# A state space layer turns its scan's inputs and outputs from SBUF to SBUF, without DRAM between

## The chip, the core and the metric

The kernel runs on one core of a Trainium2 chip. The metric is the device time of one execution in microseconds (us); a time without a unit below is in us. The core's engines are TensorE (PE, matrix products), VectorE (DVE), ScalarE (ACT), GpSimd (POOL) and SyncE (SP, which here only issues DMA transfers). Each engine works through its own instructions in order, and an instruction waits on semaphores for what it needs. A DMA is issued by an instruction on SP, ACT or POOL and is then carried out by the core's 16 DMA engines. SBUF is the memory on the core with 128 partitions, PSUM the one that PE writes to, and DRAM lies outside.

## The reference, cut to what matters

The program is a stack of layers on 512 tokens of 1024 channels in float32: a mixer of pooling and a gated delta rule, a feed-forward block, an attention layer with selected blocks, and last a state space layer with 64 groups of 16 channels and 64 complex states each. The change is in the last one:

```python
def _s5_mixer(h, w_in, log_dt, ..., d_skip, w_glu, w_out):
    u, z = jnp.split(h @ w_in, 2, axis=-1)
    u = u.astype(f32).reshape(bsz, seq, G, C)
    ...
    bu = B u                  # per group: 16 channels to 64 complex states
    x[t] = a * x[t-1] + bu[t] # the scan over the 512 tokens
    y = Re(C x) + d_skip * u
    y = jax.nn.gelu(y.reshape(bsz, seq, SSM_WIDTH))
    ga, gb = jnp.split(y @ w_glu, 2, axis=-1)
    y = ga * jax.nn.sigmoid(gb)
    y = y * jax.nn.silu(z)
    return y @ w_out
```

(The two lines on bu and x stand for several of the reference's.) The result is added to h, and a last norm follows.

## The kernel before

**Products and jobs.** All dense products go through one stream of passes (`Kit.steps`). A job is one column block of a weight matrix, 1024 by 128. It is fetched by one DMA of 512 KB (`raw`, L99, on SP's queue), split into a high and a low part (`hi` on ACT, L105, `lo` on DVE, L106), and then multiplied with the 8 tiles of the input in 24 matmuls of 128x512 (L132: per tile hi by hi, hi by lo, lo by hi). At the start of a job the one after the next is fetched, and the next one is split. What was handed to `K.after` is issued there too. In the layer the jobs are `wu` 0 to 7 (the inputs u), `wz` 0 to 7 (the gates z, whose result goes to `sz`), then 16 `wglu` and 8 `wout`. The layer begins with 70 of these matmuls (`LEAD` 36 + 34) beside the norm of the layer's input; once its factor `rstd` is there, PE goes on.

**The scan's blocks.** A block b of the eight is 128 channels, that is, one `wu` job. For each block:

- u = product times rstd (DVE L1851, `u`, 128 channels by 512 tokens). It is written to a DRAM tile `D1` (L214, issued through `K.after`), and read back in another shape by `chunks` (L1846): `Uc` has a partition for each of 8 pieces of 16 rows, and 512 values in it.
- `state(b)`: 32 short matmuls `pw` on Uc (PE L1777), and a chain on DVE (L1783 to L1796: two products m1 and m2, a sum, two scan instructions `Z`, two products m3 and m4, and a difference that gives `Xs`).
- `toeplitz(b)`: the tile `T` of the block, in 8 DMAs of 64 KB from a prepared DRAM tile `DK` (L1761), even ones on SP, odd ones on ACT.
- `output(b)`: 16 matmuls of Uc with T (PE L1810), 32 of Xs with a prepared tile `made` (PE L1817), into the bank `py`; ACT copies it to `yt` (L1819). `made` is loaded by POOL three blocks ahead.
- `finish(b)`: four transposes of yt (PE L1827), a copy `yc` (ACT L1829), and a write of yc to a DRAM tile `D2` (ACT L1830).
- `back(b)`: D2 is read into a tile `sq` of 128 by 512 (SP L1964); `outputs(b)`: GELU and a split into `yh` and `yl` (L1969), the inputs of the `wglu` products.

**What sets the order.** SP and PE run in the order in which the code is written (`MANUAL`); on DVE, ACT and POOL the scheduler of the compiler orders the instructions before the program is built. Between the steps of a block the code runs passes of the products: 384 matmuls for `wu` and `wz`, of which 70 are the lead, `SPARE` = 46 follow, `TAIL` = 24 stand behind the last block, and the rest is spread evenly over the 31 gaps between the steps. The code of block b does, in this order: chunks(b+2), state(b+1), toeplitz(b+1), a gap, the T part of output(b), a gap, its Xs part, a gap, finish(b), a gap, then back(b-1) and outputs(b-2). Ahead of block 0 stand chunks(0), chunks(1), toeplitz(0) and state(0). Buffers: three `u`, three `Uc`, two `T`, two `Xs`, three PSUM banks for products.

**Semaphores of the DMAs.** The DMAs of SP and ACT share eight semaphores in turn, so that an issue on either queue also waits until the one eight before it, over both queues together, has landed.

## Time and profile before

| | us |
|---|---|
| median of 3 runs (lowest to highest) | 1347.67 (1347.02 to 1347.9) |
| the profiled execution | 1349.54 |
| its span in the trace | 1347.4 |
| the layer's stretch in it, from the first products after the norm to the end | 1073 to 1347 |
| the eight blocks of the scan in it | 1086 to 1189 |
| first `wglu` product | 1196.5 |

The profile is a record of one execution: when each instruction began, how long it took, what the engine waited for ahead of it, and when each DMA landed. A row of a timeline has the start, the duration in us, the engine, the line, the operation, what it writes and reads, the shape and the count of instructions run together; in square brackets stands the idle time ahead of it and what ended it. The duration of a matmul is longer than the distance to the next one, since they overlap. Line numbers are those of the kernel before; in the kernel after, the same lines of the layer stand a few lower.

### The profile page before, as it was taken

To read this page: it belongs to the slowest core of one execution; us is meant where nothing else is said; L and a number is where in the kernel's file an instruction comes from. 1 tells how busy PE (TensorE), PEld (TensorE's weight loads), DVE (VectorE), ACT (ScalarE), POOL (GpSimd) and SP (SyncE) were. 2 spreads that over 40 slices of the span, in tenths; PEclk is the share of its full clock that TensorE was granted. 3 is DMA by queue.
4 is the path that set the end of the run, shared out by engine and by line. 5 is a ranking of instruction groups with operands and counts; after the bars stand their busy time and mean duration, and the time that the engine had idled before them with its cause. 6 is when DMAs were issued, how large, how long until landed. Compare 5 with 4: busy or idle time off the path is not lost.

```text
span 1347.4 us, 22525 instructions
## 1 busy us (share of the span) xinstructions
PE 1289.7 (96%) x8360; PEld 1041.2 (77%) x8360; DVE 934.4 (69%) x2163; ACT 548.1 (41%) x1167; POOL 414.5 (31%) x456
## 2 busy tenths in 40 slices
PE   8899989999998999999999999999999999899997
PEld 5677766887886888888888777887877777678896
DVE  8867785558978768768775667777876665624365
ACT  5233222334322333333434546655765322333364
POOL 5723442130015566654220003443553100003200
PEclk9899999999998999999999999999999999999998
DMA  5111101143332344444445754312005379733331
GB/s 192 42 54 33 33 32 44 48 128 98 95 141 79 127 158 144 143 144 166 141 135 157 203 163 126 95 48 79 17 18 191 104 217 282 200 100 98 94 110 63
DMA packets 81197, 152.94 MB, mean 114 GB/s; under 512 B 23840, under 2 KB 46000, under 8 KB 79936
## 3 DMA queue, kind: packets, MB, share of 16 engines
q1 hardware_dynamic: 71408, 130.46, 31.0%
q0 software_dynamic: 2688, 15.75, 3.5%
q10 hardware_dynamic: 6992, 5.30, 1.5%
q8 instruction: 66, 1.08, 0.3%
q14 instruction: 43, 0.35, 0.1%
HBM read 119.60 MB, written 21.40 MB: 105 GB/s over the span
## 4 chain that ended last, share of the span: by engine, by line
PE 75%; DVE 13%; issue 3%; DMA 3%; ACT 3%; POOL 2%; SPq 0%; DVEq 0%; ACTq 0%; POOLq 0%
PE ps L132 53%; PE ps L1886 3%; DVE lo L106 3%; PE pa L1206 3%; PE acc L1303 2%; PE pt L1264 2%; PE pv L1087 2%; DMA T<-DK 1%; DVE xlbuf L237 1%; ACT P L1215 1%; PE pb L578 1%; PE hid L1119 1%; DMA sq<-D 1%; PE py L1817 1%; PE pu L587 1%
## 5 line engine op out<-in xcount | busy, mean ns | idle before, releaser
L105 ACT CAST hi<-raw 128x512 fp32r<-128x512 f32 x357 | 203.1, 613 | 351.2 <-PE ps L132 238.1
L106 DVE TENSOR_TENSOR lo<-raw,hi 128x512 fp32r<-128x512 f32 x357 | 274.9, 795 | 80.6 <-ACT hi L105 80.3
L132 PE MATMUL ps<-xlbuf,hi 128*128 128x512 f32 x736 | 302.9, 412 | 4.4 <-DVE xlbuf L237 4.3
L132 PE MATMUL ps<-xhbuf,hi 128*128 128x512 f32 x736 | 301.9, 410 | 3.7 <-ACT hi L105 2.7
L132 PE MATMUL ps<-xhbuf,lo 128*128 128x512 f32 x736 | 299.1, 406 | 4.3 <-DVE lo L106 4.3
L132 PEld LDWEIGHTS ps<-xhbuf,hi 128*128 128x128 f32 x736 | 140.4, 191 | 38.5 <-issue 5.1
L132 PEld LDWEIGHTS ps<-xhbuf,lo 128*128 128x128 f32 x736 | 140.9, 191 | 35.4 <-DVE lo L106 6.7
L132 PEld LDWEIGHTS ps<-xlbuf,hi 128*128 128x128 f32 x736 | 140.2, 190 | 35.5 <-DVE xlbuf L237 7.2
L1220 POOL TENSOR_TENSOR P<-P,sm 128x128 f32<-128x128 f32 (+3 forms) x128 | 96.3, 773 | 189.3 <-DVE sm L1218 138.2
L132 PE MATMUL ps<-hh,hi 128*128 128x512 f32 x256 | 100.5, 393 | 0.0
L132 PE MATMUL ps<-hh,lo 128*128 128x512 f32 x256 | 99.7, 390 | 0.0
L132 PE MATMUL ps<-hl,hi 128*128 128x512 f32 x256 | 99.7, 389 | 0.0
L1215 ACT ACTIVATE P<-P,nm 128x128 f32<-128x128 f32 (+3 forms) x128 | 71.8, 563 | 57.7 <-DVE nm L1214 50.5
L1214 DVE CUSTOM_DVE_ANT_0 P<-pa,nc 128x128 f32<-128x128 f32 (+3 forms) x128 | 60.2, 484 | 9.9 <-PE pa L1206 7.5
L1644 POOL TENSOR_TENSOR F<-keep 128x512 f32<-128x512 f32 x32 | 42.0, 1334 | 80.7 <-PE pt L1672 50.4
L1644 POOL TENSOR_TENSOR V<-keep 128x576 f32<-128x576 f32 x32 | 45.3, 1436 | 35.9 <-DMA DM<-V 35.4
L132 PEld LDWEIGHTS ps<-hh,hi 128*128 128x128 f32 x256 | 48.1, 188 | 10.6 <-issue 0.8
L132 PEld LDWEIGHTS ps<-hh,lo 128*128 128x128 f32 x256 | 48.1, 188 | 10.0
L132 PEld LDWEIGHTS ps<-hl,hi 128*128 128x128 f32 x256 | 48.1, 188 | 9.7
L132 PE MATMUL ps<-yh,hi 128*128 128x512 f32 x128 | 50.6, 396 | 0.9 <-ACT hi L105 0.9
L132 PE MATMUL ps<-yh,lo 128*128 128x512 f32 x128 | 50.7, 396 | 0.0
L1264 PE MATMUL pt<-ident,P 128*128 128x128 f32 x320 | 47.1, 274 | 3.8 <-POOL P L1220 1.7
(557 smaller groups left out, 2546.8 us busy)
## 6 DMA issues: line engine op xcount, KB each, us to landing
raw<-in_wup_dram SPq DMA_DIRECT2D x32, 512.0 KB, 3.6
raw<-in_wdown_dram SPq DMA_DIRECT2D x32, 512.0 KB, 3.6
made<-DM POOLq DMA_DIRECT2D x8, 1472.0 KB, 8.1
raw<-in_win_dram SPq DMA_DIRECT2D x19, 512.0 KB, 3.5
raw<-in_s_wglu_dram SPq DMA_DIRECT2D x16, 512.0 KB, 3.5
DM<-V SPq DMA_DIRECT2D x8, 576.0 KB, 3.0
DM<-Wt SPq DMA_DIRECT2D x8, 512.0 KB, 2.9
raw<-in_n_kv_dram SPq DMA_DIRECT2D x8, 512.0 KB, 4.0
```

Source lines behind the costliest of these rows:

```text
L105: self.nc.scalar.copy(hi[:, s], raw[:, s])
L106: self.nc.vector.tensor_tensor(lo[:, s], raw[:, s], hi[:, s].bitcast(F32), ALU.subtract)
L132: mm(ps, w[:, s], xs[k][x], start=k == 0 and n == 0, stop=k == kt - 1 and n == 2)
L1087: mm(R["v"][i], x[k][:, i * 128:i * 128 + 128], w[:, s], start=k == 0 and n == 0, stop=k == 7 and n == 2)
L1206: mm(pa[g2][:, 0:lead + nk], QS[gp][:, g2, i, r, :], keys[b][:, gp * 2 + g2, key0:AT[b] + nk], start=n == 0, stop=n == 1)
L1214: v.tensor_tensor_reduce(P[g2][:, 0:nk], pa[g2][:, lead:lead + nk], pos[:, 512 - nk:512], -slope, 3e38, ALU.add, ALU.min, nm[:, g2:g2 + 1])
L1215: act.activation(P[g2][:, 0:nk], P[g2][:, 0:nk], AF.Exp, scale=-1.0, bias=nm[:, g2:g2 + 1], accum_out=sm[:, g2:g2 + 1])
L1220: p.tensor_tensor(P[g2][:, 0:nk], P[g2][:, 0:nk], sm[:, g2:g2 + 1].to_broadcast([128, nk]), ALU.mult)
L1264: nc.tensor.transpose(pt[:, s], P[g2][:, s], ident)
L1303: mm(o[halves[g2], q * 128:q * 128 + 128], Vt[:, j, c:c + 64], T[g2][:, s], start=fresh and (q, j) == (0, 0), stop=(b, q, j) == (1, 3, i), ...
L1644: eng.tensor_tensor(o[:, x:x + 4], self.S[f][:, js, b * 8 + x:b * 8 + x + 4].rearrange("p j x -> p x j")[:, :, :, None].to_broadcast([128, ...
L1886: nc.tensor.matmul(banks[m][:, 0:256], w[:, s], os[k][x][:, a * 256:a * 256 + 256], start=k == 0 and n == 0, stop=k == 7 and n == 2)
```

## The change

The DRAM tiles D1 and D2 and `chunks` go. When u of a block is there, eight DMAs on SP (through `K.after`) carry it from SBUF to SBUF: piece j takes 64 columns of all 128 partitions (32 KB) and puts them into 16 partitions of Uc. The way back is alike: `back(b)` carries yc to `sq` in eight DMAs of 32 KB on SP, from 16 partitions each; ACT no longer issues a write. `back(b)` now stands directly behind the steps of block b, and outputs(b-1) ahead of it. There are five Uc and two u instead of three each; m3 and m4 use the buffers of m1 and m2. From `wu` 4 on, the jobs of `wu` and `wz` alternate. SPARE is 36, and 8 passes (`APART`) stand between state(0) and the steps of block 0.

```diff
--- before.py
+++ after.py
@@ -1373,7 +1373,7 @@
 FIRST, EACH = 490, 60
 NORM, BACK = 20, 170
 LEAD = 36, 34
-SPARE = 46
+SPARE, APART = 36, 8
 TAIL = 24
 TWO_PI = 2.0 * math.pi
 MAGIC = 1.5 * 2.0 ** 23
@@ -1729,11 +1729,8 @@
         def pool(name, bufs, **kw):
             return stack.enter_context(tc.tile_pool(name=name, bufs=bufs, reuse_waits="tile", **kw))
 
-        self.sd = pool("sd", 1, space=bass.MemoryType.DRAM)
         self.sp = sp = pool("sp", 1)
         self.sps = pool("sps", 2, space=PSUM)
-        self.D1 = [self.sd.tile([128, 512], F32, name=f"D1{b}") for b in range(8)]
-        self.D2 = [self.sd.tile([128, 512], F32, name=f"D2{b}") for b in range(8)]
         self.sw = pool("sw", 2)
         self.rho = sp.tile([128, 64], F32, name="rho")
         nc.gpsimd.dma_start(self.rho, self.P.rho)
@@ -1788,8 +1785,8 @@
         for x in range(2):
             v.tensor_tensor_scan(Z[:, x], df, m1[:, x], 0.0, ALU.mult, ALU.add)
         X = self.Xs[b % 2]
-        m3 = sw.tile([128, 2, 256], F32, name="m3", bufs=1)
-        m4 = sw.tile([128, 2, 256], F32, name="m4", bufs=1)
+        m3 = sw.tile([128, 2, 256], F32, tag="m1", name="m3", bufs=1)
+        m4 = sw.tile([128, 2, 256], F32, tag="m2", name="m4", bufs=1)
         v.tensor_tensor(m3, Z, Cb, ALU.mult)
         v.tensor_tensor(m4, Z[:, ::-1], Sf, ALU.mult)
         m3v, m4v = (t.rearrange("p x (g n) -> p (x g) n", g=4) for t in (m3, m4))
@@ -1825,9 +1822,8 @@
         for g in range(4):
             gs = slice(g * 128, g * 128 + 128)
             nc.tensor.transpose(py[:, 1, gs], self.yt[:, gs], self.K.ident)
-        yc = sw.tile([128, 2, 4, 64], F32, name="yc", bufs=1)
-        nc.scalar.copy(yc, py[:, 1].rearrange("p (g h n) -> p h g n", g=4, h=2))
-        nc.scalar.dma_start(self.D2[b], yc.rearrange("p h g n -> p (h g n)"))
+        self.yc = sw.tile([128, 2, 4, 64], F32, name="yc", bufs=1)
+        nc.scalar.copy(self.yc, py[:, 1].rearrange("p (g h n) -> p h g n", g=4, h=2))
         yield
 
     def run(self, wcol, stack, first, last):
@@ -1841,15 +1837,14 @@
         yh, yl = (szp.tile([128, 8, 512], F32R, name=n) for n in ("yh", "yl"))
         R, held, ys, os, ga, silu, kept_w, banks, sums, got = {}, [], [], [], {}, {}, {}, {}, {}, {}
 
-        def chunks(b):
-            self.Uc[b] = self.sw.tile([128, 8, 64], F32, name="Uc", bufs=3)
-            nc.sync.dma_start(self.Uc[b].rearrange("p g n -> p (g n)"), self.D1[b])
-
         def inputs(b):
             def done(ps):
-                u = self.sw.tile([128, 512], F32, name="u", bufs=3)
+                u = self.sw.tile([128, 512], F32, name="u", bufs=2)
                 nc.vector.tensor_tensor(u, ps, R["rstd"], ALU.mult)
-                K.after(nc.sync.dma_start, self.D1[b].rearrange("(j c) (g n) -> (c g) j n", j=8, n=64), u.rearrange("p (j n) -> p j n", j=8))
+
+                self.Uc[b] = self.sw.tile([128, 8, 64], F32, name="Uc", bufs=5)
+                for j in range(8):
+                    K.after(nc.sync.dma_start, self.Uc[b][j * 16:j * 16 + 16].rearrange("p g n -> p (g n)"), u[:, j * 64:j * 64 + 64])
             return K.xs, K.hold(R, held, done)
 
         def gates(m):
@@ -1961,7 +1956,9 @@
         def back(b):
 
             y = got[b] = K.work.tile([128, 512], F32, tag="sq", name="sq")
-            nc.sync.dma_start(y.rearrange("p (j n) -> p j n", j=8), self.D2[b].rearrange("(j c) (g n) -> (c g) j n", j=8, n=64))
+            yc = self.yc.rearrange("p h g n -> p (h g n)")
+            for j in range(8):
+                nc.sync.dma_start(y[:, j * 64:j * 64 + 64], yc[j * 16:j * 16 + 16, :])
 
         def outputs(b):
 
@@ -1977,7 +1974,9 @@
                 first[b].products = [inputs(b)]
             else:
                 K.queue(W["wu"][b], [inputs(b)])
-        for m in range(8):
+            if b > 3:
+                K.queue(W["wz"][b - 4], [gates(b - 4)])
+        for m in range(4, 8):
             K.queue(W["wz"][m], [gates(m)])
         for m in range(8):
             K.queue(W["wglu"][m], [glu(m, 0)], lambda: len(ys) == 8, cut=(2, 7) if m == 0 else None)
@@ -1987,8 +1986,6 @@
         K.queue(None, [out(m, 1) for m in range(8)])
 
         def side(b):
-            if b + 2 < 8:
-                chunks(b + 2)
             if b + 1 < 8:
                 self.state(b + 1)
                 self.toeplitz(b + 1)
@@ -2003,24 +2000,20 @@
             K.lead(K.norm_steps(wcol, R, permute=True), R, held, *LEAD)
             K.norm_bank = None
             K.run(SPARE)
-            chunks(0)
-            chunks(1)
             self.toeplitz(0)
             self.state(0)
+            K.run(APART)
             steps = 8 * 4 - 1
-            left = 384 - sum(LEAD) - SPARE - TAIL
+            left = 384 - sum(LEAD) - SPARE - APART - TAIL
             for b in range(8):
                 for _ in side(b):
                     n = left // steps
                     left, steps = left - n, steps - 1
                     K.run(n)
                 if b > 0:
-                    back(b - 1)
-                if b > 1:
-                    outputs(b - 2)
-            back(7)
+                    outputs(b - 1)
+                back(b)
             K.run(TAIL)
-            outputs(6)
             outputs(7)
             self.inner.close()
             with tc.tile_pool(name="so", bufs=2, reuse_waits="tile") as so, \
```

**SP, from the end of the lead to the T tile of the second block.** Numbers behind names count tiles, and a count at the end of a row is of equal instructions in a row; DK0 belongs to block 0. Before:

```order
L214 DMA D10_10823<-u_11025 128x8x64
L214 DMA D11_10824<-u_11027 128x8x64
L214 DMA D12_10825<-u_11031 128x8x64
L99 DMA raw_11077<-in_s_wu_dram 128x1024
L214 DMA D13_10826<-u_11069 128x8x64
L1846 DMA Uc_11101<-D10_10823 128x512
L1846 DMA Uc_11103<-D11_10824 128x512
L1761 DMA T_11105<-DK0_2988 16x8x128 x4
L1846 DMA Uc_11145<-D12_10825 128x512
L1761 DMA T_11178<-DK1_2989 16x8x128 x4
```

And after:

```order
L214 DMA Uc_11009<-u_11007 16x8x64 x8
L214 DMA Uc_11012<-u_11010 16x8x64 x8
L214 DMA Uc_11017<-u_11015 16x8x64 x8
L99 DMA raw_11084<-in_s_wu_dram 128x1024
L214 DMA Uc_11077<-u_11075 16x8x64 x8
L1758 DMA T_11105<-DK0_2988 16x8x128 x4
L1758 DMA T_11184<-DK1_2989 16x8x128 x4
L99 DMA raw_11208<-in_s_wz_dram 128x1024
L214 DMA Uc_11201<-u_11199 16x8x64 x8
```

Before, one write of u of block 3 and two reads stand ahead of the four T transfers of block 0 (T_11105). After, the eight pieces of Uc of each of blocks 0 to 3 do, those of block 3 (from u_11075) right ahead of T_11105.

**DVE, from the splits beside the lead's end to the end of the first chain.** In the first rows `lo` belongs to weight jobs; ps_11044 (before) and ps_11050 (after) are the product of the fourth `wu` job. Before:

```order
L1851 TENSOR_TENSOR u_11031<-ps_10996,rstd_11023 128x512
L106 TENSOR_TENSOR lo_11034<-raw_10994,hi_11033 128x512 x2
L1851 TENSOR_TENSOR u_11069<-ps_11044,rstd_11023 128x512
L106 TENSOR_TENSOR lo_11072<-raw_11039,hi_11071 128x512 x2
L1783 TENSOR_TENSOR m1_11132<-pw_11115,made_10854 128x512
L1784 TENSOR_TENSOR m2_11133<-pw_11115,made_10854 128x512
L1785 TENSOR_TENSOR m1_11132<-m1_11132,m2_11133 128x512
L1789 SCALAR_TENSOR_TENSOR Z_11137<-dec0_10844,m1_11132 128x256 x2
L1793 TENSOR_TENSOR m3_11140<-Z_11137,made_10854 128x512
L1794 TENSOR_TENSOR m4_11141<-Z_11137,made_10854 128x512
L1783 TENSOR_TENSOR m1_11165<-pw_11148,made_10856 128x512
L1796 TENSOR_TENSOR Xs0_10847<-m3_11140,m4_11141 128x8x63
```

And after:

```order
L106 TENSOR_TENSOR lo_11019<-raw_10976,hi_11018 128x512 x2
L106 TENSOR_TENSOR lo_11079<-raw_11024,hi_11078 128x512 x2
L1843 TENSOR_TENSOR u_11015<-ps_10978,rstd_11005 128x512
L1780 TENSOR_TENSOR m1_11132<-pw_11115,made_10836 128x512
L1781 TENSOR_TENSOR m2_11133<-pw_11115,made_10836 128x512
L1782 TENSOR_TENSOR m1_11132<-m1_11132,m2_11133 128x512
L1786 SCALAR_TENSOR_TENSOR Z_11137<-dec0_10826,m1_11132 128x256 x2
L1790 TENSOR_TENSOR m3_11140<-Z_11137,made_10836 128x512
L1791 TENSOR_TENSOR m4_11141<-Z_11137,made_10836 128x512
L1793 TENSOR_TENSOR Xs0_10829<-m3_11140,m4_11141 128x8x63
L1843 TENSOR_TENSOR u_11075<-ps_11050,rstd_11005 128x512
```

Before, u of block 3 (u_11069) stands ahead of the chain of block 0 (m1_11132 to Xs0). After, it (u_11075) stands behind that chain, and u of block 2 (u_11015) behind two more splits.

**SP, at the end of the scan.** Before:

```order
L99 DMA raw_11973<-in_s_wz_dram 128x1024
L1964 DMA sq_12026<-D25_10836 128x8x64
L99 DMA raw_12046<-in_s_wglu_dram 128x1024
L1964 DMA sq_12099<-D26_10837 128x8x64
L1964 DMA sq_12104<-D27_10838 128x8x64
L99 DMA raw_12112<-in_s_wglu_dram 128x1024
```

And after:

```order
L99 DMA raw_12044<-in_s_wz_dram 128x1024
L1961 DMA sq_12099<-yc_12085 128x1x64 x8
L99 DMA raw_12123<-in_s_wglu_dram 128x1024
L1961 DMA sq_12178<-yc_12164 128x1x64 x8
L99 DMA raw_12193<-in_s_wglu_dram 128x1024
```

The second `wglu` fetch (raw_12112 before, raw_12193 after) stands behind the read of block 7 from D2 before, behind eight pieces from yc of block 7 after; between the last transposes and the first wglu pass PE has 32 passes in both.

**PE.** From the end of the lead, 44 passes stand ahead of pw of block 0 before, none between it and pw of block 1, and 7 ahead of the T part of output(0). After, the counts are 34, 8 and 7.

## Rows read from the trace of the kernel before

**Rows 1.** The page: the chain of work that ended last, shares by engine.
```profile
PE 75%; DVE 13%; issue 3%; DMA 3%; ACT 3%; POOL 2%; SPq 0%; DVEq 0%; ACTq 0%; POOLq 0%
```

**Rows 2.** Windows: stretch, its length, busy of PE, PEld, DVE, ACT, POOL; PEclk, DMA share, GB/s.
```profile
1100.00:1150.00 50.00, 47.85 (x457) 37.47 (x455) 31.58 (x50) 15.00 (x27) 2.12 (x4) 1.00 0.93 275
1200.00:1250.00 50.00, 50.00 (x216) 40.13 (x215) 18.09 (x26) 18.49 (x32) 11.88 (x9) 1.00 0.30 95
```

**Rows 3.** Waits of PE, 1084 to 1200: who waited for whom, us, times, longest.
```profile
PE py L1827 <- ACT yt L1819: 4.6, 2, 3.4
PE pw L1777 <- DVE m L1784: 1.4, 1, 1.4
PE py L1810 <- DMA T<-DK: 1.0, 1, 1.0
PE ps L132 <- ACT hi L105: 0.9, 1, 0.9
PE pw L1777 <- DMA Uc<-D: 0.8, 1, 0.8
```

**Rows 4.** Line 1761: issue time ns min/median/max, a waiter, and issue to landing.
```profile
L1761 SPq DMA_DIRECT2D T<-DK x32: 555/600/1928, 1083.1 to 1170.2; - x32
...
  ACT yt L1819: 7.2, 1
...
DMA to landing us min/median/max: 2.5/4.7/11.1
```

**Rows 5.** Timeline of PE from the restart behind the norm.
```profile
1073.09 0.73 PE L132 MATMUL ps<-xhbuf,hi 128*128 128x512 f32 x1 [0.94 <-DVE u L1851]
...
1076.61 0.39 PE L132 MATMUL ps<-xhbuf,lo 128*128 128x512 f32 x1
1076.84 0.40 PE L132 MATMUL ps<-xhbuf,hi 128*128 128x512 f32 x1
...
1085.72 1.15 PE L1777 MATMUL pw<-Uc,made 128*64 128x64 f32 x32 [0.75 <-DMA Uc<-D]
...
1091.19 1.09 PE L1810 MATMUL py<-T,Uc 128*64 128x128 f32 x16
...
1128.79 1.09 PE L1810 MATMUL py<-T,Uc 128*64 128x128 f32 x16 [0.95 <-DMA T<-DK]
...
1165.49 1.11 PE L1827 MATMUL py<-ident,yt 128*128 128x128 f32 x4 [3.37 <-ACT yt L1819]
```

**Rows 6.** Windows, columns as in rows 2: behind the restart and behind the longest wait.
```profile
1073.00:1076.50 3.50, 3.41 (x8) 2.74 (x9) 2.43 (x5) 0.34 (x1) 0.00 (x0) 0.53 0.64 157
1165.40:1168.00 2.60, 2.51 (x8) 2.22 (x9) 0.70 (x2) 0.63 (x2) 0.00 (x0) 0.50 1.19 287
```

**Rows 7.** Timeline of DVE: u of block 3, then the chain's first and last instruction.
```profile
1080.48 0.69 DVE L1851 TENSOR_TENSOR u<-ps,rstd 128x512 f32<-128x512 f32 x1 [5.05 <-PE ps L132]
...
1086.91 0.69 DVE L1783 TENSOR_TENSOR m<-pw,made 128x512 f32<-128x512 f32 x1 [4.54 <-PE pw L1777]
...
1092.08 0.67 DVE L1796 TENSOR_TENSOR Xs<-m,m 128x504 f32<-128x504 f32 x1
```

**Rows 8.** Issue time on SP by line, ns min/median/max; the attention layer's K, then D1.
```profile
L981 SPq DMA_DIRECT2D K<-hi x16: 461/594/672, 761.6 to 827.5; - x16
L214 SPq DMA_DIRECT2D D<-u x8: 360/392/1061, 1073.1 to 1122.4; - x8
```

**Rows 9.** Tile K, 760 to 830: issue to landing of transfers of 128 KB.
```profile
DMA to landing us min/median/max: 2.2/2.3/4.3
```

**Rows 10.** The chain of waits ahead of the `wglu` products: start, us, step.
```profile
1189.41 0.60 ACT yc L1829
1190.03 2.02 DMA D<-yc
...
1192.58 4.88 DMA raw<-in_s_wglu_dram
```

**Rows 11.** The page's DMA issues: count, KB each, median us to landing.
```profile
raw<-in_s_wglu_dram SPq DMA_DIRECT2D x16, 512.0 KB, 3.5
```

## The prediction

> **What bounds the kernel now.** I read the shares of the chain of waits first: PE carries 75% of it [rows 1], so a us counts where PE loses it. The layer's stretches come next: in the first 50 us behind the scan PE is busy all the time, inside the scan for 47.85 of 50, with the DMA engines at 0.93 [rows 2]. Behind the scan nothing is idle to take up a delay: what PE loses ahead of the first `wglu` product shows at the end in full. The waits of PE in the scan are few: 4.6 on the copy yt (two times, 3.4 the longest), 1.4 on DVE's m, 1.0 on T, 0.8 on Uc, and 0.9 on a weight split at the start of the `wglu` jobs [rows 3]. The clock adds to that: the granted clock is 0.50 (the 1.2 GHz level) in the 2.6 us behind the longest wait, and 0.53 behind the restart that follows the norm [rows 6]. All this is some 10 us, and so the most that the change can take away in this layer.
>
> **What is taken away.** D2's write leaves ACT, D1's reads and writes leave SP. The long yt waits come from ACT, which stood in an issue of T ahead of the copy (7.2 us put down to it [rows 4]); an issue also waits for the DMA eight before it, and D1 and D2 put large transfers among those. With pieces of 32 KB in their place, and block b's pieces ahead of T(b+2), I take these waits as gone, and also those for Uc, m and T, since pw and the T part now come at other times: 4.6 + 1.4 + 1.0 + 0.8 = 7.8 [rows 3], and half of the 2.6 us at half clock [rows 6], 1.3. **Gain 9.1**, and hardly more, as only the restart's slow start and the 0.9 are left. If the yt waits stay, 4.6 + 1.3 of it are not had (a rival, below). The products are as many as before in another order, and the gates need nothing that is late; five Uc and the shared m buffers cost nothing, as the chain writes m3 behind the sum that reads m1 and m2. Two u instead of three make u(2) wait for all pieces of Uc(0): it matters for state(2) alone, a block later, which covers it. ACT's half of T(0) has no new wait ahead of it.
>
> **What is added: a wait at the start of the scan.** This term decides. By the order of DVE, u(3) now stands behind the whole chain of state(0). By the order of SP, the eight pieces of Uc(3) stand ahead of SP's four transfers of T(0). An issue that waits holds all that is behind it, so T(0) waits for state(0), and the T part of output(0), early on PE, waits for T(0). In times of the trace of before, where the restart is at 1073.09:
>
> 1. Eight passes behind the restart take 1076.61 - 1073.09 = 3.52, the next ones 0.23 each [rows 5]. pw(0) stands behind 34: 1073.09 + 3.52 + 26 x 0.23 = 1082.6. Uc(0) is there by then: eight issues of 0.59 (below) from 1073.1 end at 1077.8, and a landing of up to 4.7 ends at 1082.5.
> 2. The chain begins 1.19 behind the start of pw (1085.72, 1086.91) and took 1092.08 + 0.67 - 1086.91 = 5.84 with an instruction of the next chain in it of 0.69 [rows 5, 7]: 5.15 without. 1082.6 + 1.2 + 5.15 = 1088.95.
> 3. u(3) takes 0.69 [rows 7]: 1089.6.
> 4. Eight issues of its pieces. No row shows such a piece. The nearest by form is a transfer on SP over all partitions in a long row of issues, K at 0.59 in the middle and 0.67 at most; the lowest is the write of u to D1 at 0.39 [rows 8]. I take 0.59, nearest in that many follow each other: 4.7, with 3.1 and 5.4 as ends. 1094.3.
> 5. T's four issues: the last begins 3 x 0.60 later [rows 4]: 1096.1.
> 6. Landing: at least 2.5, in the middle 4.7 [rows 4]; the middle comes from blocks with full DMA engines. I take 3.3, since SP has only eight small pieces out there: 1099.4, with 1096.9 and 1101.5 as ends.
> 7. PE is at the T part after pw(0) (1.15), 8 passes (1.84), pw(1) (1.15) and 7 passes (1.61) [rows 5]: 1082.6 + 5.75 = 1088.35.
>
> **The wait is 1099.4 - 1088.35 = 11.1**, with ends 8.6 and 13.1. Behind a wait of 3.37 the granted clock was 0.50 [rows 5, 6], and eight passes behind the restart lost 3.52 - 8 x 0.23 = 1.7. I take **1.7** for the start behind the new wait, from 1.3 (half of 2.6) to 3.4 (twice 1.7, as the pause is longer). Later blocks inherit SP's late pieces, but PE is late by the same 11 us.
>
> **The way back at the end.** In before, yc of block 7 ends at 1190.01, and the second `wglu` fetch is issued at 1192.58, after D2's write of 2.02 and the read; it takes 4.88 [rows 10], and its split ends PE's wait of 0.9. After, eight pieces of 0.59 stand ahead of that fetch, 4.7 instead of 2.57, and the fetch takes 3.5 in the middle of all its kind [rows 11]; between 3.5 and 4.88 I take 4.2. The wait grows by 2.15 - 0.7 = **1.5**, from -0.8 (3.1 and 3.5; the 0.9 is then all but gone) to 2.8 (5.4 and 4.88). The pieces for other blocks are issued while PE has a block's passes ahead of it.
>
> **The sum.** -9.1 + 11.1 + 1.7 + 1.5 = +5.2. Ends: -9.1 + 8.6 + 1.3 - 0.8 = 0.0, and -9.1 + 13.1 + 3.4 + 2.8 = +10.2. The profiled execution took 1349.54, 1.9 above the median of the runs, so the next one would take 1354.7; on the median of 1347.67 it is **1352.9**, from 1347.7 to 1357.9.
>
> **The rivals.**
>
> *Short issues: faster.* If an issue from SBUF to SBUF cost next to nothing, u(3) would hardly hold T(0). With 0.1 for each of the twelve and a landing of 2.5, T lands at 1089.6 + 0.8 + 0.3 + 2.5 = 1093.2, the wait is 4.9, and the sum -9.1 + 4.9 + 1.3 - 0.8 = -3.7: 1344.0. It decides below about 0.2 per issue, from which the sum is -2.7. Against it: no issue in the rows is under 0.36 [rows 8]. For it: that these transfers touch no DRAM, and none of the trace is of that kind.
>
> *The yt waits stay: slower.* ACT still issues half of T ahead of its copies, each behind the DMA eight before it. If that still lands late, 5.9 of the gain is missing: 1358.8.
>
> *SP's queue becomes the bound: slower.* A block takes (1128.79 - 1091.19) / 3 = 12.5 on PE [rows 5]. SP now has 8 + 8 + 4 issues and a fetch in a block: at 0.59 it is 12.4, at 0.67 14.1. Some four blocks have pieces in both directions, so at 0.67 PE waits up to 4 x 1.6 = 6.4: 1359.3. Against it: blocks without a new Uc have 12 issues and catch up.
>
> *Pieces in a row one after the other: slower.* The pieces of K are issued each 0.6 us and land after 2.3 [rows 8, 9], so several are under way at once. If those of Uc(3) were not, eight would take 18.4 in place of 4.7, and the sum would be +18.9: 1366.6. The Trainium skill has a rule by which the change is the wrong way round: its page "DMA: Bandwidth & Descriptors", section "Rules for kernel authors", wants many small transfers put together into one large one, since under 64 KB most of the time is overhead. By that rule 32 KB pieces are too small; the K rows agree on the landing, but not that it adds up piece by piece, as the issues overlap it.
>
> **How the numbers follow.** The forecast has 0.76, short issues 0.10, yt waits 0.06, SP's queue 0.05, pieces in a row 0.03. 0.2% is 2.7 us, about what a measurement of this kernel can tell from no change. Of the forecast's range, the part from 1347.7 to 1350.4 is within that; it needs low ends of most terms, and I give it 0.18 of the 0.76. Faster: 0.10. Same: 0.18. Slower: 0.58 + 0.06 + 0.05 + 0.03 = 0.72. The range is the forecast's, with the yt rival at its top and some spread of runs below: 1347.0 to 1359.0. It leaves out short issues, pieces in a row and most of SP's queue, 0.18.
>
> **What would show it.** In the profile after, PE's timeline has one wait of 8 to 13 us ahead of the first T part, named T, near 1088, and a granted clock near 0.5 behind it; DVE shows u(3) behind Xs(0), and SP four T issues behind eight of Uc. The waits for yt are gone, and the wait on the split at the `wglu` start is 1 to 4. The forecast is wrong if T(0) lands by 1094, if yt waits of several us stand in PE's list again, or if T, Uc or sq end waits of PE in blocks 1 to 4, which would be SP's queue.

## The result, and the profile after

The changed kernel takes 1382.02 us in the median of 4 runs (1380.52 to 1386.1), beside 1347.79 for the kernel before (1347.02 to 1349.61): 1.0251 times as long, with an interval of 1.0232 to 1.0271. That is 34 us more, where 5 were forecast and 11 was the upper end. The profiled execution took 1380.52, with a span of 1378.4, 31.0 above that of before.

Where the 31.0 are: PE's restart behind the norm stands at 1075.25 instead of 1073.09 [rows 5], a difference of 2.2 that comes from stages ahead of the change and is of the size by which runs of one kernel differ. From there to the first `wglu` pass it is 151.1 (1226.38) instead of 123.4 (1196.5), 27.7 more, and from there to the end 1.1 more. So the loss is in the scan. The windows over the scan, first of the kernel before, then after (stretch, length, busy of PE, PEld, DVE, ACT, POOL, granted clock as a share of full, DMA share, GB/s):

```profile
1073.00:1197.00 124.00, 116.22 (x987) 91.41 (x987) 70.21 (x113) 35.27 (x63) 2.69 (x5) 0.97 0.77 215
```

```profile
1075.00:1227.00 152.00, 120.99 (x987) 95.13 (x987) 71.68 (x113) 35.08 (x62) 2.68 (x5) 0.90 0.53 143
```

The same 987 matmuls. PE's idle time is 152.00 - 120.99 = 31.0 instead of 7.8, 23.2 more, and the same work is busy for 4.8 more, at a granted clock of 0.90 instead of 0.97. (In this execution the granted clock behind the restart is 1.00, where it was 0.53 before [rows 6]. Only before has that slow start, 1.7 in the prediction, so the half clock behind the new waits costs more than the 4.8.) The DMA engines have less to do on the mean, 0.53 instead of 0.77, so mean bandwidth isn't what bounds the scan; what the large loads do to single transfers is another matter, and is tried below.

Who made PE wait in the scan (us, times, longest; compare rows 3):

```profile
PE py L1807 <- DMA T<-DK: 29.1, 5, 12.3
PE ps L132 <- ACT hi L105: 2.2, 1, 2.2
PE pw L1774 <- DVE Z L1786: 1.6, 1, 1.6
```

The waits of 4.6 for yt are gone. In their place T comes late five times, also in blocks 2 and 3, which the prediction names as a sign of SP's queue. PE's timeline has the five, in blocks 0, 2, 3, 5 and 6:

```profile
1103.34 1.97 PE L1807 MATMUL py<-T,Uc 128*64 128x128 f32 x16 [12.34 <-DMA T<-DK]
...
1131.72 1.09 PE L1807 MATMUL py<-T,Uc 128*64 128x128 f32 x16 [1.27 <-DMA T<-DK]
...
1151.49 1.98 PE L1807 MATMUL py<-T,Uc 128*64 128x128 f32 x16 [7.26 <-DMA T<-DK]
...
1184.22 1.97 PE L1807 MATMUL py<-T,Uc 128*64 128x128 f32 x16 [5.49 <-DMA T<-DK]
...
1200.87 1.92 PE L1807 MATMUL py<-T,Uc 128*64 128x128 f32 x16 [2.76 <-DMA T<-DK]
```

Behind the long ones the same 16 matmuls last 1.92 to 1.98 instead of 1.09; in the 3 us behind the longest the granted clock is 0.50, the 1.2 GHz level (a window, columns as above):

```profile
1103.00:1106.00 3.00, 2.66 (x18) 2.26 (x19) 0.00 (x0) 0.00 (x0) 0.00 (x0) 0.50 0.75 177
```

The first wait was forecast, at 11.1 (8.6 to 13.1). The other four, 16.8 together, were not. SP's timeline shows how they come about, here for T of block 0 and for that of block 3:

```profile
1075.28 16.59 SPq L214 DMA_DIRECT2D Uc<-u  x24
1091.97 0.53 SPq L99 DMA_DIRECT2D raw<-in_s_wu_dram  x1
1092.59 5.05 SPq L214 DMA_DIRECT2D Uc<-u  x8
1097.68 5.47 SPq L1758 DMA_DIRECT2D T<-DK  x8
```

```profile
1132.05 0.33 SPq L99 DMA_DIRECT2D raw<-in_s_wz_dram  x1
1132.47 6.27 SPq L214 DMA_DIRECT2D Uc<-u  x8
1138.85 7.64 SPq L1961 DMA_DIRECT2D sq<-yc  x8
1146.59 2.52 SPq L1758 DMA_DIRECT2D T<-DK  x4
```

Before, three issues stood between a fetch and the next T at that place; now there are 16, and T's issue at 1146.59 comes 14.5 behind the fetch. PE wanted that T at 1151.49 - 7.26 = 1144.23. Of the 14.5, 16 issues at 0.64 (below) are 10.3. The issues themselves, by line (ns, min/median/max), and the landing of the pieces of u:

```profile
L214 SPq DMA_DIRECT2D Uc<-u x64: 547/597/1602, 1075.3 to 1189.5; - x64
...
DMA to landing us min/median/max: 1.9/2.1/9.5
```

The duration of an issue, 0.6, is the one that I took (0.59). But from one issue to the next it is 0.64, as 8 in 5.05 show (7 distances of 0.64 and one duration). And SP waited in front of some:

```profile
SPq L214 <- DMA T<-DK: 12.8, 5, 6.0
SPq L99 <- DMA T<-DK: 8.3, 3, 7.7
...
SPq L1961 <- DMA Uc<-u: 2.8, 2, 2.1
```

The rows with "DMA" are put down to waits for the DMA eight before, on SP's or ACT's queue: 12.8 + 8.3 + 2.8, and 2.9 in smaller rows, 26.8 in the scan (a wait of 2.6 for a `wglu` fetch at its end is left out). All of it lies between 1100.7, the first issue for T of block 1, and 1207.0, the end of the last for T of block 7. SP makes 116 issues there, 74 at 0.64 each; with the 26.8 that is 101. PE needs 92 from its T part of block 0 (1103.3) to that of block 7 (1211.7) without the waits for T. So the issues alone would fit, and issues and waits together don't. The chain of waits (start, us, step) leads through such waits to SP's issue of T of block 3:

```profile
1123.81 9.95 DMA T<-DK
1133.77 0.59 SPq L214
...
1136.33 8.31 DMA Uc<-u
1145.25 0.60 SPq L1961
...
1146.59 2.84 DMA T<-DK
```

One T transfer of ACT took 9.95 to land, and a piece of Uc on SP waited for it; a piece of Uc took 8.31, against 2.1 in the middle, and a piece of sq waited for that; T came behind. On the way from the fetch at 1132.05 to this T, SP waited 7.7 ahead of the fetch, 0.7 and 2.1 for landings, 10.5 together. Landings as long as these go with the loads of `made` (1472 KB each): without them (an experiment below) the longest of a piece of u is 5.6 instead of 9.5.

### The profile page after: what moved, and what is told of

The parts are those of the page before. It is cut to its first block, busy times and chain, and to the rows that moved or that the text cites. A ratio compares the mean times of both kernels' runs of the same rounds, so it can differ in the third digit from the quotient of the medians.

```text
span 1378.4 us, 22681 instructions
## 1 busy us (share of the span) xinstructions
PE 1294.4 (94%) x8360; PEld 1044.6 (76%) x8360; DVE 935.8 (68%) x2163; ACT 548.6 (40%) x1167; POOL 414.2 (30%) x456
## 4 chain that ended last, share of the span: by engine, by line
PE 72%; DVE 12%; DMA 5%; SPq 4%; issue 3%; ACT 2%; POOL 2%; DVEq 0%; ACTq 0%; POOLq 0%
PE ps L132 51%; PE ps L1881 3%; DMA T<-DK 3%; PE pa L1206 2%; PE acc L1303 2%; DVE lo L106 2%; PE pt L1264 2%; SPq L214 2%; PE pv L1087 2%; SPq L1961 1%; ACT P L1215 1%; PE hid L1119 1%; DVE xlbuf L237 1%; PE pb L578 1%; DVE cacc L456 1%
## 5 line engine op out<-in xcount | busy, mean ns | idle before, releaser
L132 PEld LDWEIGHTS ps<-xhbuf,lo 128*128 128x128 f32 x736 | 140.8, 191 | 35.6 <-DVE lo L106 6.7
L132 PEld LDWEIGHTS ps<-hh,hi 128*128 128x128 f32 x256 | 48.1, 188 | 10.5 <-issue 0.8
```

Of the source, the lines that this page charges most:

```text
L132: mm(ps, w[:, s], xs[k][x], start=k == 0 and n == 0, stop=k == kt - 1 and n == 2)
```

## The experiments

Three theories were put against each other. **Order theory**, the prediction's: T of block 0 is late because its issues wait for u(3) behind DVE's chain. **Queue theory**: SP issues one DMA in 0.64 us, and there are too many. **Ring theory**: SP waits for landings through the eight semaphores that it shares with ACT. All ratios are to the kernel before in runs on the same chip; differences in us between two kernels go by their medians, and the kernel before had medians from 1347.14 to 1349.66 on those chips.

**Three u buffers.**

```diff
-                u = self.sw.tile([128, 512], F32, name="u", bufs=2)
+                u = self.sw.tile([128, 512], F32, name="u", bufs=3)
```

> The changed kernel with three u buffers instead of two: u of block 3 then stands ahead of DVE's chain of block 0, as it did in the kernel before. Order theory (mine of the prediction: T of block 0 is late because its issues wait for u of block 3 behind the chain): SP's pieces follow each other without that pause, PE's first wait for T, 12.3 us in the changed kernel, falls by 5 us or more, the time to 1377 or less. Queue theory (32 pieces at 0.64 us stand ahead of T of block 0, 20.5 us from the first u on, so that u of block 3 is there by the time SP comes to it): the wait falls by 1.5 us at most, the time stays within 1380 to 1384. Both leave the later waits for T (16.8 us) as they are.

Measured: 1384.32, ratio 1.0274 (1.0241 to 1.0307). The time is 0.3 above the queue theory's range. u(3) is early, and the first wait stays: DVE's u(3) at 1082.24 is ahead of the chain's first product at 1083.77, the pieces on SP and PE's wait are as they were.

```profile
1082.24 0.69 DVE L1843 TENSOR_TENSOR u<-ps,rstd 128x512 f32<-128x512 f32 x1
1083.77 0.69 DVE L1780 TENSOR_TENSOR m<-pw,made 128x512 f32<-128x512 f32 x1 [0.84 <-PE pw L1774]
```

```profile
1074.61 16.66 SPq L214 DMA_DIRECT2D Uc<-u  x24
...
1091.99 5.04 SPq L214 DMA_DIRECT2D Uc<-u  x8
1097.08 5.46 SPq L1758 DMA_DIRECT2D T<-DK  x8
```

```profile
1102.69 1.98 PE L1807 MATMUL py<-T,Uc 128*64 128x128 f32 x16 [12.30 <-DMA T<-DK]
```

The order theory falls. SP comes to the pieces of u(3) at 1092, because 24 others (16.6 together) and a fetch are ahead of them; u(3) was there in both kernels.

**One transfer instead of eight pieces, both ways.** The turn is left out, values land in the wrong places; bytes, producers and consumers are as in the changed kernel. The rows get longer too, 2 KB instead of 256 bytes.

```diff
-                for j in range(8):
-                    K.after(nc.sync.dma_start, self.Uc[b][j * 16:j * 16 + 16].rearrange("p g n -> p (g n)"), u[:, j * 64:j * 64 + 64])
+                K.after(nc.sync.dma_start, self.Uc[b].rearrange("p g n -> p (g n)"), u)
...
-            yc = self.yc.rearrange("p h g n -> p (h g n)")
-            for j in range(8):
-                nc.sync.dma_start(y[:, j * 64:j * 64 + 64], yc[j * 16:j * 16 + 16, :])
+            nc.sync.dma_start(y, self.yc.rearrange("p h g n -> p (h g n)"))
```

> The changed kernel with one transfer of 256 KB, 128 rows of 2 KB, from SBUF to SBUF in place of each eight pieces of 32 KB, both ways. It leaves out the turn itself: values land in the wrong places, the bytes and the waits on producers and consumers are those of the changed kernel. Queue and ring theories (what costs is the number of DMAs): the waits for T and the late split at the wglu start go, SP issues 14 times 0.64 us less per block, time 1340 to 1348. If instead the transfer from SBUF to SBUF or the moved order of the steps is what costs, it stays above 1365.

Measured: 1343.87, ratio 0.9961 (0.9946 to 0.9976). All waits for T are gone; PE's list from 1074 to 1200 is:

```profile
PE py L1824 <- ACT yt L1816: 4.5, 3, 3.0
PE ps L132 <- DVE lo L106: 0.2, 1, 0.2
```

So with one DMA in place of eight all of the loss goes, 38 us, and the rest of the change, without the turn, is a gain of 4. Some waits for yt are there again. SP still waits 24.4 for DMAs in this scan, about as long as in the changed kernel (29.4 by the same count, with the 2.6), and T transfers land after up to 13.0; but SP has 61 issues in the scan instead of 173, and PE never waits for T. So long waits for landings did no harm on a queue that had time for them. The run doesn't separate the number of DMAs from the length of their rows; the next one and the landings of 2.1 speak for the number.

**Twice as many pieces of u**, 16 of 16 KB instead of 8 of 32 KB.

```diff
-                    K.after(nc.sync.dma_start, self.Uc[b][j * 16:j * 16 + 16].rearrange("p g n -> p (g n)"), u[:, j * 64:j * 64 + 64])
+                    for i in range(2):
+                        K.after(nc.sync.dma_start, self.Uc[b][j * 16:j * 16 + 16, :, i * 32:i * 32 + 32], u[:, j * 64 + i * 32:j * 64 + i * 32 + 32])
```

> The changed kernel with 16 pieces of 16 KB for each u instead of 8 of 32 KB: the same bytes, 64 issues more. Queue theory: an issue costs 0.64 wherever SP is the bound, which it is for most of the scan, so 64 x 0.64 = 41 more at most; the first wait grows by 32 x 0.64 = 20 and the rest by 10 to 20: 1412 to 1424. If SP's time goes mostly into waits for landings, not into issues, the smaller pieces land sooner and the time grows by under 20: below 1402.

Measured: 1419.8, ratio 1.0515 (1.0493 to 1.0537), 37.8 more than the changed kernel by the medians (35.6 by the two ratios), for 64 issues of the same bytes: 0.56 to 0.59 each. That is within the queue theory's range. The first wait is 19.8 instead of 12.3, not 20 more; but PE also waits for Uc ahead of it, so that the T part of block 0 begins 48.5 behind the restart (1125.05 - 1076.54) instead of 28.1: 20.4 later for 32 more issues, 0.64 each. An issue of 16 KB lasts as long as one of 32 KB:

```profile
PE py L1807 <- DMA T<-DK: 41.8, 5, 19.8
PE pw L1774 <- DMA Uc<-u: 13.0, 3, 5.1
```

```profile
L214 SPq DMA_DIRECT2D Uc<-u x128: 547/597/1736, 1076.6 to 1228.7; - x128
```

Nearly each added issue reaches the end at its full length: from here on SP's queue bounds the scan.

**Without the loads of `made` in the scan**, blocks 3 to 7 computing with the tiles of blocks 0 to 2.

```diff
-        V = self.made.pop(b)[1]
+        self.old = self.made.pop(b)
+        V = self.old[1]
...
-                self.load(b + 3)
+                self.made[b + 3] = self.old
```

> The changed kernel without the loads of made (1472 KB each, by POOL) for blocks 3 to 7: those blocks compute with the tiles of blocks 0 to 2. All pieces and issues stay. Queue theory (issues of 0.64 us, 20 in a block, are too many): the later waits for T (16.8 us) stay at 12 or more, time 1374 to 1382. Ring theory (an issue waits until the DMA eight before it has landed, and landings of 8 to 10 us beside the loads of made are what holds SP): the later waits fall under 5 us, and the half clock behind them with it, time 1362 to 1370. Both leave the first wait of 12.3 us.

Measured: 1370.13, ratio 1.0165 (1.0134 to 1.0197), 11.9 less than the changed kernel, between the two expectations and past the lower end of the queue's. T is waited for 17.0 in four places with 10.5, the first, the longest, so the later waits are 6.5 instead of 16.8; a wait of 3.5 for yt is new. The landings beside the large loads are a third of the whole loss, but 10.3 of the 16.8 that the prediction didn't have; the first wait stands without them.

**ACT's half of T issued by POOL**, which takes it out of the ring.

```diff
-            (self.K.nc.scalar if j % 2 else self.K.nc.sync).dma_start(T[j * 16:...
+            (self.K.nc.gpsimd if j % 2 else self.K.nc.sync).dma_start(T[j * 16:...
```

> The changed kernel with the four T transfers of a block that ACT issues given to POOL. SP's 20 issues in a block stay, but SP and ACT's ring of eight semaphores holds SP's transfers alone. Queue theory: the time stays at 1376 to 1386, the first wait and later ones for T stay above 20 in sum. Ring theory: SP's waits for T transfers (21 us in the changed kernel) go, PE's later waits fall from 16.8 to 8 or less: 1364 to 1372.

Measured: 1375.28, ratio 1.0204 (1.0166 to 1.0241), 7 less than the changed kernel (the intervals of the two ratios overlap), and between the two again: the waits for T are 22.3, which is above the 20 of the queue theory, 9.5 of it the first, so the later ones are 12.8 instead of 16.8. SP's waits for T transfers are gone from its list. What SP and ACT owe to each other in the ring is some of the loss, and not the larger part.

**T of block 0 issued ahead of the lead.**

```diff
+            self.toeplitz(0)
             K.lead(K.norm_steps(wcol, R, permute=True), R, held, *LEAD)
...
-            self.toeplitz(0)
             self.state(0)
```

> The changed kernel with the eight T transfers of block 0 issued ahead of the lead, instead of behind the pieces of blocks 0 to 3. All theories: PE's first wait for T (12.3 us) is gone with the half clock behind it (1.5 us), unless another takes its place. If the later waits are each due to SP's rate (queue theory: 16 pieces and 4 T issues at 0.64 us, 12.8 us, in a block of 12.5 us of PE), part of the gain is given back, since SP was 12 us behind PE at that point and PE's wait gave it time: the later waits grow from 16.8 to 20 to 28 us, time 1372 to 1380. If each later wait is due to something of its own block (slow landings beside the loads of made), they stay at 16.8, time 1367 to 1370.

Measured: 1382.22, ratio 1.0251 (1.0219 to 1.0283): no gain at all. The first wait is gone, and the others are 22.6 in six places. The waits are those of the first case, and the time is 2 above it. About half of the gain, 5.8 of 12.3, goes back into the waits for T of later blocks; 1.9 for Uc and 1.3 for a split are new. In the profiled execution the scan is 148.0, 3.1 less than in the changed kernel, and the rest of the span is 3.0 more, which this change doesn't explain.

```profile
PE py L1807 <- DMA T<-DK: 22.6, 6, 7.3
```

**Each half of the change alone.** With u by pieces and yc through DRAM as before (of the two edits the added lines alone, cut):

```diff
+        self.D2 = [self.sd.tile([128, 512], F32, name=f"D2{b}") for b in range(8)]
...
+        nc.scalar.dma_start(self.D2[b], self.yc.rearrange("p h g n -> p (h g n)"))
...
+            nc.sync.dma_start(y.rearrange("p (j n) -> p j n", j=8), self.D2[b].rearrange("(j c) (g n) -> (c g) j n", j=8, n=64))
```

> The changed kernel with the way back as before: ACT writes yc to DRAM, one transfer on SP reads it into sq. Only u goes by pieces. Queue theory: 32 pieces still stand ahead of T of block 0, so PE's first wait of 12 us stays; later SP has 14 issues of 0.64 in a block of 12.5 (9.0 us), so the later waits for T fall from 16.8 to 5 or less and the late split at the wglu start to 1; time 1360 to 1367. Ring theory: the reads of 256 KB land late and stand among the eight, later waits stay at 8 or more, time 1368 to 1378.

With yc by pieces and u through DRAM:

```diff
+        self.D1 = [self.sd.tile([128, 512], F32, name=f"D1{b}") for b in range(8)]
...
+            self.Uc[b] = self.sw.tile([128, 8, 64], F32, name="Uc", bufs=5)
+            nc.sync.dma_start(self.Uc[b].rearrange("p g n -> p (g n)"), self.D1[b])
...
+                K.after(nc.sync.dma_start, self.D1[b].rearrange("(j c) (g n) -> (c g) j n", j=8, n=64), u.rearrange("p (j n) -> p j n", j=8))
```

> The changed kernel with the way in as before: u is written to DRAM in one transfer and read back into Uc in one, in the order of issues of the kernel before. Only yc goes by pieces. Queue theory: few issues stand ahead of T of block 0, so the first wait is gone; SP has 15 issues in a block (9.6 us of 12.5); at the end eight pieces still stand ahead of the second wglu fetch, a wait of 2.2 there. Time 1346 to 1354. If both halves share the loss (ring theory, since each block still sends 8 pieces, T and the DRAM transfers through the same eight semaphores), waits for T or Uc of 8 or more in the scan and 1356 to 1366.

Measured: 1371.72 with u's pieces, 1.017 (1.0145 to 1.0196), and 1365.87 with yc's, 1.0126 (1.0094 to 1.0159). Both times are over the queue theory's and within the ring theory's; the waits with u's pieces, 7.8 behind the first, are just under the 8 of the ring theory. PE's waits for DMAs, the longest in total with u's pieces, then both rows with yc's:

```profile
PE py L1809 <- DMA T<-DK: 19.8, 3, 12.0
```

```profile
PE pw L1776 <- DMA Uc<-D: 11.5, 3, 5.8
PE py L1809 <- DMA T<-DK: 5.4, 2, 4.5
```

With 14 or 15 issues in a block, 9 to 10 us, SP has time for its issues on average, and PE waits all the same: an issue that waits holds those behind it. With yc's pieces, SP waits 10.7 for yc itself, since the pieces of block b now stand ahead of the read of Uc and of T of later blocks.

**The reordering alone**, on the kernel before (alternating jobs, 36 + 8 passes, back(b) directly behind block b):

> The kernel before with the reordering of the change alone: gates alternate with inputs, 36 + 8 passes ahead of block 0, outputs(b-1) and then back(b) directly behind block b. u and yc go through DRAM as before. If the pieces are the whole loss, as the single transfers suggest (1344 in the changed order): 1340 to 1350. If the new place of back(b) holds SP by itself (its read waits for the yc of the same block and for the write to DRAM, and Uc and T of the next block stand behind it): PE waits for Uc or T of 8 or more in the scan, 1354 to 1366, and then part of the loss of the two half changes is the order's.

Measured: 1351.66, ratio 1.0025 (1.001 to 1.004). The reordering isn't free, but it is a tenth of the loss; it lies between the two cases, nearer to the first.

**Pieces issued by POOL instead of SP**, once those of yc, once those of u (`nc.gpsimd.dma_start` in the respective line):

> The changed kernel with the pieces of yc issued by POOL instead of SP. Queue theory: SP has 13 issues in a block (8.3 us of 12.5); the first wait of 12 us stays, the later ones fall under 4, and the second wglu fetch has no pieces ahead of it; time 1358 to 1366. Rival: a piece costs POOL more than 1.5 us, so eight and the load of made behind them take a block's time, and PE waits for made or for sq instead: above 1370.

> The changed kernel with the pieces of u issued by POOL instead of SP. T of block 0 then has no pieces ahead of it on SP: the first wait of 12.3 for T is gone by any theory. Queue theory: SP has 13 issues in a block, the later waits for T fall under 4. On POOL the 32 pieces of blocks 0 to 3 stand in a row: at 0.64 each (as on SP) those of block 1 are there by 1088 and PE waits 2 at most, time 1348 to 1356; at 1 us each or more, pw of blocks 1 and 2 wait 5 to 15 us for Uc, and Uc of later blocks stands behind loads of made that wait for PE, time 1358 to 1375.

Measured: 1374.02 with yc's on POOL, 1.0185 (1.0154 to 1.0216), and 1369.05 with u's, 1.0151 (1.0114 to 1.0188). They are better than the changed kernel by 8 and 13, and neither is as good as the queue theory has it, though its waits came true: with yc's on POOL T is waited for 12.1 and then 3.5. Both times lie in the ranges of the slow-POOL cases, but not for their reason: an issue of a piece takes POOL 0.52 to 0.60, where those cases had 1.5 and 1 us. With yc's, 5.7 of waits for a weight split stand beside the T waits. With u's, the T waits are gone altogether, and PE waits 2.2 for Uc; 9.4 of waits for yt stand in their place:

```profile
PE py L1824 <- ACT yt L1816: 9.4, 3, 5.0
```

In the longest of them ACT's copy stands behind a step (`dec`, L1767) that waits 3.99 for DVE's scan. In both kernels the end of the program is longer too: from PE's last instruction to the end it takes 10.6 instead of 6.9, since POOL's closing DRAIN takes 9.3 instead of 4.1 (changed kernel, then yc's on POOL; ns min/median/max):

```profile
L2138 POOLq DRAIN  x3: 46/93/4066, 1372.0 to 1378.1; - x3
```

```profile
L2138 POOLq DRAIN  x3: 46/93/9300, 1360.3 to 1370.1; - x3
```

These 3.7 were in no theory.

**T of block 0 early, and yc's pieces on POOL.**

> The changed kernel with T of block 0 issued ahead of the lead and the pieces of yc issued by POOL: 13 issues in a block on SP. With SP's slack the first wait of 12 us, now gone, isn't given back if SP's rate was the reason: 1374 (yc's pieces on POOL alone) less 12 and the half clock behind it, 1357 to 1363. If something else gives it back, it stays above 1368.

Measured: 1371.25, ratio 1.0172 (1.014 to 1.0203), only 3 below the kernel with yc's pieces on POOL, which is not clear of noise. So the second case came true: SP's rate alone doesn't explain why the gain is given back. PE's waits in the scan are 19.2 in sum here and 23.0 there: those for T went from 15.6 to 8.7, and those for Uc, yt and splits grew. The chain of waits shows one place where it goes:

```profile
1097.83 7.63 DMA made<-DM
...
1105.73 3.17 DMA sq<-yc
...
1108.97 1.28 ACT L1966
...
1110.93 3.10 DMA T<-DK
...
1114.10 0.57 SPq L214
...
1117.92 8.07 DMA Uc<-u
1126.01 3.22 DMA T<-DK
```

By this chain the last piece of sq waits on POOL for the landing of a load of `made`, ACT's GELU (L1966) for the pieces, ACT's T behind the GELU, a piece of Uc on SP for that T to land, and the next T for that piece. With T, u and yc on three queues, ACT and the rings still tie them to one another. How much of the 12 us goes this way was not measured.

**A version that beats both.** Before the change SP and ACT were held by the four DRAM trips of a block; the two halves and the single transfers suggest that what helps is few DMAs in their ring. So in the kernel before the four trips were given to POOL, in one run all four, in another those of yc alone (`nc.gpsimd.dma_start` at L214's call in `inputs`, L1846, L1830 and L1964; at L1830 and L1964).

> The kernel before with the four DRAM trips of a block (u out and in, yc out and in) issued by POOL, nothing else changed. Ring theory: the transfers of 256 KB leave the eight semaphores that SP and ACT share, ACT no longer stands in an issue of T ahead of yt, and the waits of 4.6 for yt go; time 1340 to 1346. Rival: on POOL the reads wait for the landing of their writes, with the loads of made behind them, and PE waits for Uc or made by 5 us or more: 1350 to 1365.

> The kernel before with the write and the read of yc's DRAM tile issued by POOL, u's by SP as before. Ring theory: 1342 to 1347, as half of the large transfers leave the ring, and those that keep SP waiting longest. Rival as in the run with all four on POOL, but smaller: 1348 to 1356.

Measured: 1343.58, ratio 0.9954 (0.9937 to 0.9972), with all four, and 1346.38, ratio 0.9978 (0.9966 to 0.9989), with yc's, both as the ring theory has it. PE's waits in the scan with all four:

```profile
PE ps L132 <- ACT hi L105: 2.2, 1, 2.2
PE pw L1777 <- DVE m L1784: 1.4, 1, 1.4
```

The waits for yt, T and Uc [rows 3] are gone, and the scan has 113.6 from the restart to the first `wglu` pass instead of 123.4. Not all of the 9.8 is the edit's: the slow start behind the restart (0.53 [rows 6], 1.7) isn't in this execution, whose granted clock there is 1.00, and behind the scan it takes 3.4 more, where the wait for the split is 2.2 instead of 0.9. By the medians 5 us are left. It is the fastest of the kernels here that compute the whole. Why the waits for yt go was not tried by itself.

## Why the prediction was wrong

**The sign and the first wait** were as forecast: slower, one wait ahead of the first T part of 12.3 (forecast 11.1), half clock behind it, and on the split at the `wglu` start 2.2 (forecast 0.9 + 1.5). **The reason for the first wait was not.** Steps 2 to 4 of the sum put SP's pieces of u(3) behind DVE's chain. They begin at 1092.6 in the kernel after because 24 pieces, 16.6 together, and a fetch are ahead of them; with three u buffers u(3) is 6.8 earlier, counted from the restart, and the wait is the same. The two paths end 2 us from each other, so the size came out right for a wrong reason, by luck. The sum priced the eight pieces of u(3) and those of u(0), and never the 16 between. "ACT's half of T(0) has no new wait ahead of it" was wrong too: in the ring each of its four issues stands eight behind a piece of u(3), and the first of them came at 1096.45, 0.02 after that piece had landed, instead of 1080.26 (after, then before):

```profile
1096.45 0.58 ACTq L1758 DMA_DIRECT2D T<-DK  x1
```

```profile
1080.26 0.58 ACTq L1761 DMA_DIRECT2D T<-DK  x1
```

The last of ACT's half lands at 1102.67 and the last of SP's at 1103.10, so either half alone would have made nearly the same wait.

**The gains** of 9.1 came only in part: the waits for yt and Uc are gone, 5.4; a wait of pw of 1.6 stands in place of one of 1.4; T's wait didn't go but grew. The single transfers show 1343.87, 4 below the kernel before, though some yt waits were left there.

**The step that failed** is the sentence that SP's late pieces don't matter in later blocks, "but PE is late by the same 11 us", with the rival that SP's queue becomes the bound, at 0.05 and 6.4 at most. It cost 16.8 in four waits, and their half clock, where the sum had nothing. Three things were wrong in it.

- The unit. I multiplied by the duration of an issue (0.59), where the distance from one to the next counts, 0.64. At 0.59 a block's 20 issues and a fetch are 12.4, which fits into 12.5; at 0.64 they are 13.4 and don't. The row of durations [rows 8] doesn't say this; the starts in a timeline do. By itself this is a small error: 0.9 in each of some four blocks, and the rival had allowed for 1.6 at 0.67.
- The waits in the queue. I let an issue wait for the DMA eight before it when I explained the old yt waits, and not for the new pieces. SP spent 26.8 of the scan so, which with 74 of issues is more than PE's 92. This is the part that the sum and the rival both lacked: without the loads of `made` 10.3 of the 16.8 go, and 11.9 of the time. It did harm only with the many issues: the kernel with single transfers has nearly the same waits on SP and no wait for T.
- The head of the line. "Blocks without a new Uc have 12 issues and catch up" takes a queue as a mean. On the mean the issues do fit. But SP issues in program order: fetch, pieces of u, pieces of yc, T. A fetch that waited 7.7 for a T transfer to land, until 1132.05, had 16 issues between itself and T of block 3, which came 14.5 later, and PE was idle for 7.26.

**The rival of pieces in a row**, at 0.03, was set aside since landings overlap. They do overlap: eight pieces were issued in 5.05 and landed after 2.1 each in the middle. But issues on one queue don't, and the single transfers took away all of the loss. The Trainium skill, page "DMA: Bandwidth & Descriptors", section "Rules for kernel authors", asks for one large transfer instead of many small ones. That advice holds here, though the loss is in the queue that issues and not in landings added up piece by piece.

**What stays open.** How the 34 us divide between issues and landings isn't settled to better than this: with one transfer for eight, 38 less; without the loads of `made`, 12 less; with ACT's T out of the ring, 7 less; and these overlap. T of block 0 issued early gave nothing, and how its 12.3 are lost again is shown for about half. The two halves alone cost 22 and 16, together more than the whole, so they aren't separate terms. That eight semaphores rather than some other limit make the issues wait was read from the program and from issues like ACT's above, which follow such a landing at once, and tried only by taking transfers out of the ring; no run with more semaphores was made. Of the waits for yt with u's pieces on POOL only the longest was followed.

## What to carry to other kernels

Before replacing one DMA by several, count the issues of its queue in one period of the loop, times the distance between starts in a timeline, add what the queue spends waiting for landings, and hold the sum against the period. Here 74 of issues fitted into PE's 92, and with 27 of waits they didn't; past that point each further issue reached the end nearly at full length, 0.56 to 0.59 of 0.64. Then walk the queue in program order and ask, for each transfer that a busy engine waits for, how many issues stand between it and the last one that had to wait. And a detour through DRAM that nobody waits for is cheap: to move it to POOL's queue gave 1343.58 here, and to shorten it, in single transfers without the turn, 1343.87.

## What the runs showed of the hardware that was not expected

- An issue on SP lasts 0.597 in the middle for 16 KB, 0.597 for 32 KB and 0.599 for 64 KB, with 0.64 from start to start. The single transfers of 256 KB take 0.518. More bytes don't make it longer in these forms.
- A piece of 32 KB from SBUF to SBUF lands after 2.1 in the middle and 1.9 at least, but after 8.31 in the chain above, and up to 9.5; without the loads of `made`, up to 5.6.
- The DMA engines were at 0.53 on the mean in the slower scan and 0.77 in the faster one: the slower scan had mean bandwidth left.
- With 64 pieces issued by POOL, POOL's DRAIN at the end of the program took 9.3 instead of 4.1, and the program ended 3.7 later behind PE's last instruction.
